# Layer B's shared values: each matmul over 128 contraction rows becomes two over 64, in banks of their own

## The chip, the core and the metric

The kernel runs on one core of one Trainium2 chip. Its engines work side by side and meet at semaphores: PE (TensorE) multiplies, and loads its stationary operand with separate instructions (PEld); ScalarE is ACT in the profile, VectorE DVE, GpSimd POOL, and SP issues the transfers of weights. The metric is the device time of one execution in microseconds; smaller is better.

## The reference, cut to what matters

The model is a two-layer encoder trunk over 256 tokens of width 2048. Layer A is a chunked softmax attention beside an attention into 256 memory tokens, then an MLP with squared ReLU. After it one key and one value projection are made for layer B, whose stick-breaking attention uses them:

```python
kv = rms_norm(h, norm_kv) @ w_kv_shared          # [256, 2048] @ [2048, 3072]
k_sb = split_heads(kv[..., :W_MAIN], N_HEADS_MAIN)   # 12 heads of 128
v_sb = split_heads(kv[..., W_MAIN:], N_HEADS_MAIN)   # 12 heads of 128
```

The change concerns `v_sb` alone: a product of [256, 2048] with [2048, 1536], scaled for each token by the inverse root of its mean square.

## The kernel before, in words

All weights pass once through the chip as a stream of 512 KB pieces, called half-units here. `prepare` (L135) loads one, ACT rounds it to float32r (`hi`, L150) and DVE takes the rest of it (`lo`, L151); four buffers hold each of them. The activations are split in the same way, so a product is the sum of three matmuls: hi by hi, hi by lo, lo by hi. All of these have one line in the profile, L56, since a helper issues PE's instructions in the order in which they are written. The order on ACT, DVE and POOL is set by a scheduler that works with estimated times.

`tokens_major` (L190) makes 512 columns for all 256 tokens. It has a PSUM bank for each of the two tiles of 128 tokens (m = 0, 1) and goes over eight half-units; each holds two tiles of 128 contraction rows. For each of these and each m there are three matmuls with 512 moving columns, so a group has 96. The stationary operand is the activations (`kvx`), the moving one the weights. The banks come from `ps_mm` (L98), which has four, the tiles `acc`; so one group's banks are emptied while the next group fills the other two.

Layer B's shared values (L820 to L825) are three such groups. Ahead of them stands the last down projection of layer A's MLP, behind them the shared keys; both go by `features_major` (L233), one bank for each output tile, emptied by ACT (`low`, L259) and DVE (`dn`, L732, or `sc`, L830). `value_heads` (L380) empties a value group: ACT reads a bank, multiplies by the token's factor `r` and writes the SBUF tile `vb` (L383). Within the first group stand a few small matmuls of two side tasks: `stat` (sums of squares) and `spread` (the factors on all partitions).

Of the kernel before, what the change touches and what calls it, by code (L numbers as in the profile page):

```python
# [16 lines left out]
P = 128  # L17
# [12 lines left out]

# Columns of the small per-partition parameters.
G_ATTN0, G_ATTN1, G_MEM0, G_MEM1, G_MLP0, G_MLP1, G_KV = (16 * i for i in range(7))
G_QK = 7 * 16
N_SMALL = G_QK + 6

# The order of contraction tiles in the output projection: memory heads first.
WO_ORDER = [12, 13, 14, 15] + list(range(12))
AHEAD = 3
# Output tiles of the output projection that begin before the last heads are done.
FIRST = 4  # L40
# Tiles of hidden features that begin before the last residual tile is done.
FIRST_UP = 2
# [3 lines left out]
class InOrder:  # L46
    """An engine whose instructions are issued in the order in which they are written."""

# [20 lines left out]
def trunk(  # L69
# [32 lines left out]

# [1 line left out]
    nc.scalar.preload_act_table_set("natural_log_exp_and_others")  # L104
    # The tensor engine's clock rises while it works: it multiplies zeros until the data arrive.
    zeros = wide.tile([P, 512], F32, name="zeros", tag="wide")
# [11 lines left out]
    neg_tri = const.tile([P, P], F32, name="neg_tri")  # L118
    # neg_tri[k, s] = -1 where k >= s
    nc.gpsimd.affine_select(  # L120
        out=neg_tri[:], in_=neg_ones[:], pattern=[[-1, P]], compare_op=ALU.is_ge,
        fill=0.0, base=0, channel_multiplier=1,
    )
    # Exact in float32r: the sums that they make of a split operand are float32's.
    neg_tri_r = const.tile([P, P], F32R, name="neg_tri_r")
# [3 lines left out]

# [1 line left out]
    stream = []  # L131
# [28 lines left out]

# [1 line left out]
    waiting = deque()  # L162
# [27 lines left out]
    def tokens_major(act, evacuate):  # L190
        """Eight half-units of 512 columns: out[tokens, 512] for both tiles of tokens."""
        banks = [ps_mm.tile([P, 512], F32, name="acc", tag="acc") for _ in range(2)]
        for half in range(8):
            hi, lo = weights()
            for k2 in range(2):
                kt = 2 * half + k2
                h512 = hi[:, k2 * 512 : (k2 + 1) * 512]
                l512 = lo[:, k2 * 512 : (k2 + 1) * 512]
                for m in range(2):
                    a_hi = act[:, kt, m * P : (m + 1) * P]  # L200
                    a_lo = act[:, kt, T + m * P : T + (m + 1) * P]
                    mm(banks[m][:], a_hi, h512, kt == 0, False)
                    mm(banks[m][:], a_hi, l512, False, False)
                    mm(banks[m][:], a_lo, h512, False, kt == KT - 1)
            if half == 7:
                evacuate(banks)
            slot()

    def half_unit(bank, act, order, first, last):
        hi, lo = weights()  # L210
        for k8 in range(8):
            kt = order[k8]
            w = slice(k8 * P, (k8 + 1) * P)
            mm(bank[:], hi[:, w], act[:, kt, :], first and k8 == 0, False)
            mm(bank[:, T:], lo[:, w], act[:, kt, :T], False, last and k8 == 7)

    def one_bank(act, evacuate):
        """As features_major, all parts in the same columns."""
        bank = ps_mm.tile([P, 512], F32, name="acc", tag="acc")
        for half in range(2):  # L220
            hi, lo = weights()
            for k8 in range(8):
                kt = 8 * half + k8
                w = slice(k8 * P, (k8 + 1) * P)
                mm(bank[:, :T], hi[:, w], act[:, kt, :T], kt == 0, False)
                mm(bank[:, :T], hi[:, w], act[:, kt, T:], False, False)
                mm(bank[:, :T], lo[:, w], act[:, kt, :T], False, kt == KT - 1)
            if half == 0:
                slot()
        evacuate(bank)  # L230
        slot()

    def features_major(act, evacuate, order=tuple(range(KT))):  # L233
        """Two half-units of 128 columns: out[features, tokens], and beside it its low part."""
        bank = ps_mm.tile([P, 512], F32, name="acc", tag="acc")
        half_unit(bank, act, order[:8], True, False)
        slot()
        half_unit(bank, act, order[8:], False, True)
        evacuate(bank)
        slot()  # L240

    def halves_first(act, n, evacuate, order=tuple(range(KT)), between=None):
        """n tiles as of features_major, of all of them the first half before the second."""
        banks = []
        for _ in range(n):
            bank = ps_mm.tile([P, 512], F32, name="acc", tag="acc")
            half_unit(bank, act, order[:8], True, False)
            banks.append(bank)
            slot()
        if between is not None:  # L250
            between()
        for i in range(n):
            half_unit(banks[i], act, order[8:], False, True)
            evacuate(i, banks[i])
            slot()
# [5 lines left out]

# [1 line left out]
    def pin(ins, pinned=True):  # L263
        """Work that could be done early, and would then hold up what is more urgent."""
        if pinned:
            tc.keep_in_program_order(ins)

    def split_scaled(dst, kt, src, gain, pinned=False):
        """dst[:, kt] = the high and the low part of src * gain."""
        g = sm[:, gain + kt : gain + kt + 1]  # L270
# [26 lines left out]
    def token_stats(acc, name):  # L297
        """Per token, on partitions: mean square + eps, and its inverse root."""
        ps = ps_y.tile([P, 512], F32, name="stat", tag="y")
# [12 lines left out]
    def spread(r, scale, name):  # L312
        """r of a token, on all partitions along the free dimension."""
        ps = ps_y.tile([P, 512], F32, name="spread", tag="y")
# [10 lines left out]
    def inverse_square(acc, name):  # L325
        """1 / (mean square + eps) of a token, on all partitions."""
        ps = ps_y.tile([P, 512], F32, name="inv", tag="y")
# [6 lines left out]
    def normed_heads(banks, eps_ms, gain, dst):  # L334
        """Four heads of a QK-normed projection: dst[d, head, token]."""

# [54 lines left out]
    def soft_tail(p, spans, rs, vt, j, y, head, ready=None, lag=1):  # L391
        """Normalise p[q, k], transpose it, and weigh the values with it. spans: of each tile of
        queries, its columns in p."""
        for m, (lo, hi) in enumerate(spans):
            nc.vector.tensor_scalar_mul(p[:, lo:hi], p[:, lo:hi], rs[:, m : m + 1])
        n = spans[-1][1]
        tp = None
        blocks = []  # (key tile, query tile, columns in p)
        for m, (lo, hi) in enumerate(spans):
# [80 lines left out]
    def strict(t):  # L480
        """Keep t[s, t] where s < t, in the two diagonal blocks of [0:256 | 128:256]."""
        v = t.rearrange("p (b t) -> p b t", t=P)[:, 0:3:2, :]
# [56 lines left out]

# [1 line left out]
    def wide_group(w):  # L541
# [45 lines left out]

# [1 line left out]
    def spaced(fn, n, per, start=0):  # L589
# [10 lines left out]
    def later(fn, n):  # L600
        """fn, n slots from now."""

# [75 lines left out]

    # q's gains carry the scores' scale
    gq = const.tile([P, 3], F32, name="gq")  # L680
# [5 lines left out]
    def out_proj(l, y, resid, done):  # L686
        """h = resid + y @ w_o, in place in resid; done(o) follows each tile of features."""

# [60 lines left out]

# [1 line left out]
    def x_stat_side():  # L751
# [7 lines left out]
    for j in range(NM):  # L759
        queue_side(mem_head(qm, km[0], vm[0], j, y, 2), 4)  # L760
    # The values come last: only their weighing is left when the last group is done.
    for i in range(3):
# [42 lines left out]

# [1 line left out]
    qx = new_act("qx")  # L807
# [14 lines left out]
    for g in range(3):  # L822
        v_ = heads4(f"vb{g}")
        tokens_major(kvx["xg"], lambda b: value_heads(b, bst["r"], v_))
        vb.append(v_)  # L825
# [15 lines left out]
    for hd in range(NH):  # L841
        q = nar.tile([P, T], F32, name=f"qb{hd}", tag="qb", bufs=3)
        features_major(qx, lambda b: scaled(b, q[:], bst["rbs"]))
        # The last heads are due sooner.
        wait, *lags = (1, 2, 2) if hd < NH - 2 else (0, 2, 2) if hd < NH - 1 else (0, 2, 1)
# [17 lines left out]
def _wide(w):  # L863
    """[2048, n] -> [n / 512, 8, 128, 1024]: of 512 columns, two tiles of rows."""
    k, n = w.shape
# [3 lines left out]
def _narrow(w, order=None):  # L869
    """[k, n] -> [n / 128, k / 1024, 128, 1024]: of 128 columns, eight tiles of rows."""  # L870
    k, n = w.shape
# [6 lines left out]
def _tokens(x):  # L878
    """[256, 2048] -> [4, 128, 1024]: features on partitions, four tiles of them a chunk."""
    return x.T.reshape(4, 4, P, T).transpose(0, 2, 1, 3).reshape(4, P, 1024)  # L880
# [45 lines left out]
```

## Time and profile before

| | |
|---|---|
| time, median of 3 runs | 2241.86 us (2240.25 to 2244.43) |
| the profiled execution: span from first to last instruction | 2249.5 us |
| PE busy | 2233.1 us, 99% |
| DVE, ACT, POOL busy | 58%, 48%, 29% |
| DMA | 184 GB/s mean |
| the three groups of shared values in the span | 1175.09 to 1241.31 us |

The profiled execution has no time beside its span; the span is 7.6 us (0.34%) above the median of the runs, and nothing is known of it outside the span. The span counts from the first to the last instruction. A timeline row gives start, duration, engine, line, operation and how many were merged; in brackets stands the idle time of the engine before it and what ended that. The ends of matmuls are modelled, so the distance between two starts (the pitch) tells what one costs in a stream, and not its duration.

### The profile page before, as it was taken

Reading aid. Unit: us, or ns where it says so; the run is one execution under the profiler, and the core shown is the slowest. Engines: PE = TensorE matmul, PEld = TensorE weight load, DVE = VectorE, ACT = ScalarE, POOL = GpSimd, SP = SyncE. Lnnn points to the kernel's source line nnn. Section 1 sums busy time; section 2 is a strip of 40 time slices with the busy share of each in tenths; the row PEclk is TensorE's granted clock in tenths of the full one; section 3 lists DMA queues with packets and bytes.
Section 4 is the critical chain, followed back from the end, with each engine's and each line's share of the span. In section 5 each row is a group of like instructions: output and inputs, shape, how many; then the busy total and the mean of one; then the engine's idle time right before and its main releaser. Section 6 shows DMA issues by size and latency. Waiting matters only on the chain.

```text
span 2249.5 us, 31961 instructions
## 1 busy us (share of the span) xinstructions
PE 2233.1 (99%) x12208; PEld 1921.3 (85%) x12208; DVE 1304.7 (58%) x1574; ACT 1075.6 (48%) x1572; POOL 652.9 (29%) x662
## 2 busy tenths in 40 slices
PE   8999999999999999999999999999999999999999
PEld 6888888888888888888888888888888888888888
DVE  8755556665555555555665455576555555555554
ACT  6545455544444444444455447554444444444443
POOL 6610112622222222222460112362222222222222
PEclk9999999999999999999999999999999999999999
DMA  7555555555555555555555553455555555555553
GB/s 282 189 176 160 181 177 201 191 187 186 187 187 181 186 187 187 185 185 186 183 188 189 188 185 132 141 196 184 183 186 187 187 182 187 186 185 187 187 194 134
DMA packets 117225, 414.76 MB, mean 184 GB/s; under 512 B 13136, under 2 KB 16720, under 8 KB 117072
## 3 DMA queue, kind: packets, MB, share of 16 engines
q1 hardware_dynamic: 116496, 410.63, 55.0%
q8 instruction: 95, 1.56, 0.3%
q10 hardware_dynamic: 576, 2.10, 0.3%
q14 instruction: 58, 0.48, 0.1%
HBM read 410.58 MB, written 2.10 MB: 183 GB/s over the span
## 4 chain that ended last, share of the span: by engine, by line
PE 97%; issue 1%; DVE 1%; POOL 1%; ACT 0%; DMA 0%; SPq 0%
PE acc L56 94%; PE yp L56 1%; PE tp L56 1%; PE z L56 1%; PE s L56 1%; POOL hid L720 1%; DVE mg L273 0%; DVE lo L151 0%; DMA raw<-in_w_mem 0%; ACT hi L150 0%; ACT hid L719 0%; PE stat L56 0%; PE inv L56 0%; PE spread L56 0%; DVE dn L740 0%
## 5 line engine op out<-in xcount | busy, mean ns | idle before, releaser
L151 DVE TENSOR_TENSOR lo<-raw,hi 128x1024 fp32r<-128x1024 f32 (+1 forms) x771 | 981.3, 1273 | 846.0 <-ACT hi L150 845.4
L150 ACT CAST hi<-raw 128x1024 fp32r<-128x1024 f32 (+1 forms) x771 | 807.2, 1047 | 1117.9 <-PE acc L56 643.3
L56 PE MATMUL acc<-hid,hi 128*128 128x512 f32 (+1 forms) x2064 | 725.3, 397 | 3.5 <-POOL hid L720 3.5
L56 PE MATMUL acc<-mlpx,hi 128*128 128x512 f32 x2048 | 723.9, 399 | 0.0
L56 PE MATMUL acc<-hid,lo 128*128 128x256 f32 x2048 | 575.2, 281 | 0.0
L56 PE MATMUL acc<-mlpx,lo 128*128 128x256 f32 x2048 | 574.9, 281 | 0.0
L56 PEld LDWEIGHTS acc<-hid,hi 128*128 128x128 f32 x2064 | 386.7, 188 | 100.9 <-POOL hid L720 6.1
L56 PEld LDWEIGHTS acc<-mlpx,hi 128*128 128x128 f32 x2048 | 384.8, 188 | 95.7
L56 PEld LDWEIGHTS acc<-hid,lo 128*128 128x128 f32 x2048 | 386.9, 189 | 0.0
L56 PEld LDWEIGHTS acc<-mlpx,lo 128*128 128x128 f32 x2048 | 386.8, 189 | 0.1
L720 POOL TENSOR_TENSOR hid<-upsq,hid 128x256 fp32r<-128x256 f32 x128 | 186.2, 1455 | 546.6 <-ACT hid L719 546.6
L733 POOL TENSOR_TENSOR dn<-dn,r_mlp 128x256 f32<-128x256 f32 x127 | 93.9, 739 | 477.0 <-DVE dn L732 477.0
L56 PE MATMUL acc<-hi,xg 128*128 128x512 f32 x640 | 210.5, 399 | 0.0
L56 PE MATMUL acc<-y,hi 128*128 128x512 f32 x512 | 179.0, 395 | 0.0
L56 PE MATMUL acc<-y,lo 128*128 128x256 f32 x512 | 141.9, 277 | 0.0
L56 PEld LDWEIGHTS acc<-hi,xg 128*128 128x128 f32 x640 | 120.2, 188 | 24.6
L56 PE MATMUL acc<-lo,xg 128*128 128x512 f32 x320 | 124.7, 390 | 0.0
L259 ACT COPY low<-acc 128x256 f32<-128x256 f32 x311 | 113.7, 366 | 4.4 <-PE acc L56 4.4
L56 PEld LDWEIGHTS acc<-y,hi 128*128 128x128 f32 x512 | 96.0, 188 | 21.8
L734 POOL TENSOR_TENSOR h<-h,dn 128x256 f32<-128x256 f32 x127 | 93.7, 738 | 10.0
L56 PEld LDWEIGHTS acc<-y,lo 128*128 128x128 f32 x512 | 96.2, 188 | 0.1
L56 PE MATMUL acc<-hi,mg 128*128 128x512 f32 x256 | 82.1, 398 | 2.1 <-ACT hi L150 1.4
(154 smaller groups left out, 1820.5 us busy)
## 6 DMA issues: line engine op xcount, KB each, us to landing
raw<-in_w_up SPq DMA_DIRECT2D x256, 512.0 KB, 3.4
raw<-in_w_down SPq DMA_DIRECT2D x256, 512.0 KB, 3.3
raw<-in_w_in SPq DMA_DIRECT2D x80, 512.0 KB, 3.4
raw<-in_w_o SPq DMA_DIRECT2D x64, 512.0 KB, 3.4
raw<-in_w_mem SPq DMA_DIRECT2D x29, 512.0 KB, 4.1
raw<-in_w_kv_v SPq DMA_DIRECT2D x24, 512.0 KB, 3.4
raw<-in_w_kv_k SPq DMA_DIRECT2D x24, 512.0 KB, 3.4
raw<-in_w_q SPq DMA_DIRECT2D x24, 512.0 KB, 3.3
```

Of the source, the lines that this page charges most:

```text
L56: return self._tc.keep_in_program_order(fn(*args, **kwargs))
L150: nc.scalar.copy(hi[:, part], raw[:, part])
L151: nc.vector.tensor_tensor(lo[:, part], raw[:, part], hi[:, part].bitcast(F32), op=ALU.subtract)
L259: nc.scalar.copy(low[:], bank[:, T:])
L720: nc.gpsimd.tensor_tensor(hid[:, f, T:], a[:], hid[:, f, :T].bitcast(F32), op=ALU.subtract)
L733: nc.gpsimd.tensor_tensor(t[:], t[:], inv["r2"][:], op=ALU.mult)
L734: nc.gpsimd.tensor_tensor(h(o), h(o), t[:], op=ALU.add)
```

## The change

For the three groups of shared values `tokens_major` is replaced by `tokens_major_rows`, and `value_heads` by `value_heads_rows`. The new loop takes four banks. Each former matmul becomes two: one multiplies the upper 64 contraction rows (partitions 0 to 63) and writes banks 0 or 1 (for m = 0, 1), the other the lower 64 (partitions 64 to 127) and writes banks 2 or 3. Each of them still has 512 moving columns and a stationary operand of 128 columns. To empty them, ACT scales a lower bank into an SBUF tile `vpart`, and DVE scales the upper bank and adds `vpart`. The diff also takes out comments and docstrings, which changes no instruction; line numbers grow by up to 34.

```diff
+    def tokens_major_rows(act, evacuate):
+        banks = [ps_mm.tile([P, 512], F32, name="acc", tag="acc") for _ in range(4)]
+        rows = (slice(0, 64), slice(64, P))
+        for half in range(8):
+            hi, lo = weights()
+            for k2 in range(2):
+                kt = 2 * half + k2
+                cols = slice(k2 * 512, (k2 + 1) * 512)
+                for m in range(2):
+                    a_hi = slice(m * P, (m + 1) * P)
+                    a_lo = slice(T + m * P, T + (m + 1) * P)
+                    for a, w, first, last in (
+                        (a_hi, hi, kt == 0, False),
+                        (a_hi, lo, False, False),
+                        (a_lo, hi, False, kt == KT - 1),
+                    ):
+                        for u, r in enumerate(rows):
+                            mm(banks[2 * u + m][:], act[r, kt, a], w[r, cols], first, last)
+            if half == 7:
+                evacuate(banks)
+            slot()
+
+    def value_heads_rows(banks, r, dst):
+        for m in range(2):
+            s = r[:, 2 * m : 2 * m + 1]
+            part = wide.tile([P, 512], F32, name="vpart", tag="wide")
+            nc.scalar.activation(part[:], banks[2 + m][:], AF.Copy, scale=s)
+            nc.vector.scalar_tensor_tensor(
+                out=dst[:, m * 512 : (m + 1) * 512], in0=banks[m][:], scalar=s, in1=part[:],
+                op0=ALU.mult, op1=ALU.add,
+            )
...
-        tokens_major(kvx["xg"], lambda b: value_heads(b, bst["r"], v_))
+        tokens_major_rows(kvx["xg"], lambda b: value_heads_rows(b, bst["r"], v_))
```

The order of instructions and the semaphores that they wait on show where a bank is waited for. First PE at the start of the first group, behind the last matmuls of the down projection (`hid`), before the change:

```order
L56 MATMUL acc<-hid_3_9059,lo_10695 128x256
L56 MATMUL acc<-hi_10716,kvx 128x512 [waits Activation_49]
L56 MATMUL acc<-lo_10717,kvx 128x512 [waits DVE_49]
L56 MATMUL acc<-hi_10716,kvx 128x512
L56 MATMUL acc<-hi_10716,kvx 128x512 [waits PE_49]
L56 MATMUL acc<-lo_10717,kvx 128x512
```

And with the change:

```order
L56 MATMUL acc<-hid_3_9059,lo_10695 128x256
L56 MATMUL acc<-hi_10716,kvx 128x512 [waits Activation_49]
L56 MATMUL acc<-hi_10716,kvx 128x512 [waits DVE_49,PE_49]
L56 MATMUL acc<-lo_10717,kvx 128x512 [waits DVE_49]
L56 MATMUL acc<-lo_10717,kvx 128x512
L56 MATMUL acc<-hi_10716,kvx 128x512 x2
L56 MATMUL acc<-hi_10716,kvx 128x512 [waits DVE_49] x2
L56 MATMUL acc<-lo_10717,kvx 128x512 x2
```

The seventh and the eighth matmul (m = 1, upper and lower rows) now wait on DVE: their banks are those of the last two tiles of the down projection, which `dn` on DVE empties. Before, the group took the other two banks. (The shape printed is that of the output.)

Second, PE at the start of the second group with the change:

```order
L56 MATMUL acc<-hi_10948,kvx 128x512 x2
L56 MATMUL acc<-hi_10980,kvx 128x512 [waits Activation_49]
L56 MATMUL acc<-hi_10980,kvx 128x512 [waits DVE_49]
L56 MATMUL acc<-lo_10981,kvx 128x512 x2
L56 MATMUL acc<-hi_10980,kvx 128x512 x2
L56 MATMUL acc<-hi_10980,kvx 128x512 [waits Activation_49]
L56 MATMUL acc<-hi_10980,kvx 128x512 [waits DVE_49]
```

For each m the upper rows get a bank that ACT has read in the first group, and the lower rows one that DVE has read. Before, the second group began so:

```order
L56 MATMUL acc<-hi_10898,kvx 128x512
L56 MATMUL acc<-hi_10918,kvx 128x512 [waits Activation_49]
L56 MATMUL acc<-lo_10919,kvx 128x512 [waits DVE_49]
L56 MATMUL acc<-hi_10918,kvx 128x512 x2
L56 MATMUL acc<-lo_10919,kvx 128x512
```

There the waits are those for `hi` and `lo` of the half-unit.

Third, DVE at the end of the first group, before and with the change (`qx` is the split of layer B's queries' input):

```order
L322 TENSOR_SCALAR rbs_b<-rb_b 128x256
L151 TENSOR_TENSOR lo_10950<-raw_10948,hi_10949 128x1024
L273 SCALAR_TENSOR_TENSOR qx<-h_3119,sm,qx 128x256
L151 TENSOR_TENSOR lo_10970<-raw_10968,hi_10969 128x1024
L273 SCALAR_TENSOR_TENSOR qx<-h_3119,sm,qx 128x256
```

```order
L356 TENSOR_SCALAR rbs_b<-rb_b 128x256
L151 TENSOR_TENSOR lo_11024<-raw_11022,hi_11023 128x1024
L307 SCALAR_TENSOR_TENSOR qx<-h_3119,sm,qx 128x256
L151 TENSOR_TENSOR lo_11056<-raw_11054,hi_11055 128x1024
L238 SCALAR_TENSOR_TENSOR vb_10805<-acc,r_b,vpart 128x512 x2
L307 SCALAR_TENSOR_TENSOR qx<-h_3119,sm,qx 128x256
```

The two additions stand right behind the `lo` of a half-unit, where DVE had nothing of the group's end before. On ACT the two reads of the lower banks stand where the two reads of `value_heads` stood.

## The prediction

> **What bounds the kernel now.** First the page: the shares of the engines, and the shares of the chain of work that ended last.
>
> ```profile
> span 2249.5 us, 31961 instructions
> PE 2233.1 (99%) x12208; PEld 1921.3 (85%) x12208; DVE 1304.7 (58%) x1574; ACT 1075.6 (48%) x1572; POOL 652.9 (29%) x662
> PE 97%; issue 1%; DVE 1%; POOL 1%; ACT 0%; DMA 0%; SPq 0%
> ```
>
> PE is the bound, and the chain lies on it. Then whom PE waits for, over the whole span:
>
> ```profile
> PE acc L56 <- DVE lo L151: 5.6, 5, 2.3
> PE acc L56 <- POOL hid L720: 3.5, 8, 0.4
> PE cold L56 <- DVE zeros L107: 1.5, 1, 1.5
> PE acc L56 <- ACT hi L150: 1.4, 1, 1.4
> PE acc L56 <- ACT mg L271: 0.7, 1, 0.7
> ```
>
> That is 12.7 us, and no row is a wait for a PSUM bank. So whatever PE loses in the changed stage is lost at the end, and only what PE does there can win. Then what a matmul of that stage costs, from PE's timeline in the second and third group and at the keys behind them:
>
> ```profile
> 1217.74 0.39 PE L56 MATMUL acc<-lo,kvx 128*128 128x512 f32 x1
> ...
> 1219.33 0.62 PE L56 MATMUL acc<-hi,kvx 128*128 128x512 f32 x2
> 1219.78 0.39 PE L56 MATMUL acc<-lo,kvx 128*128 128x512 f32 x1
> ...
> 1241.31 0.39 PE L56 MATMUL acc<-kvx,hi 128*128 128x512 f32 x1
> ...
> 1241.65 0.40 PE L56 MATMUL acc<-kvx,hi 128*128 128x512 f32 x1
> ```
>
> From 1217.74 to 1219.78 there are nine matmuls: 2.04 / 9 = 226.7 ns each, the pitch, whatever the 0.39 us of a record. In the keys a matmul of 512 columns and one of 256 take 1241.65 - 1241.31 = 0.34 us together here (0.35 us further on), so 256 columns cost some 120 ns: a matmul is about 107 ns for each 256 columns and some 13 ns that do not grow with them.
>
> **The change part by part.** *The rate.* 288 matmuls of 128 rows become 576 of 64 rows with the same 512 columns. If the upper and the lower half of the array run at the same time, a pair costs one pitch; if not, two. No row of the trace has a matmul of 64 rows, so the bounds are these. Below: the fixed 13 ns vanish for each of 288 pairs, -3.7 us. Above: twice the pitch, 288 x 0.2267 = +65.3 us. Between them lies the load of the stationary operand, of which there are now two in a pitch. Its price shows where the moving operand is tiny, with two columns:
>
> ```profile
> 1185.75 0.39 PE L56 MATMUL acc<-hi,kvx 128*128 128x512 f32 x1
> 1185.98 0.50 PE L56 MATMUL stat<-ones,kvsq 128*128 128x2 f32 x4
> 1186.34 0.48 PE L56 MATMUL acc<-hi,kvx 128*128 128x512 f32 x1
> 1186.66 0.39 PE L56 MATMUL acc<-lo,kvx 128*128 128x512 f32 x1
> ```
>
> Four loads with their tiny matmuls take 1186.34 - 1185.98 = 0.36 us, 90 ns each. Two make 180 ns, below the pitch of 227 ns, so they fit if they are loaded beside the streaming, as they are now:
>
> ```profile
> 1198.02 0.39 PE L56 MATMUL acc<-lo,kvx 128*128 128x512 f32 x1
> 1198.02 0.41 PEld L56 LDWEIGHTS acc<-hi,kvx 128*128 128x128 f32 x2
> ```
>
> The load for the next matmul starts with the matmul before it, on the same 128 rows. The Trainium skill, "TensorE: Matmul & The Clock Gate", Part 3 (the mechanism), says that matmuls on different row groups overlap, started some 4 ns apart; no row here can show it. The same place says that a load overlaps a matmul in flight only when the row groups differ; the two rows above disagree, for the undivided array. I take one pitch for a pair, a rate term of 0: the streams lie on separate rows and separate banks, the instructions of a pair are adjacent, and two loads fit. If loads do not quite hide, two of them with the cost of 120 ns that the matmul of 256 columns bounds make 240 ns: 13 x 288 = +3.8 us, the upper end of this case.
>
> *The waits for banks.* A group now takes all four, so nothing covers the emptying. What ACT and DVE do at the three starts and at the start of the keys:
>
> ```profile
> 1175.17 1.06 ACT L150 CAST hi<-raw 128x1024 fp32r<-128x1024 f32 x1 [0.84 <-PE acc L56]
> 1176.12 0.36 ACT L259 COPY low<-acc 128x256 f32<-128x256 f32 x1
> ...
> 1197.37 1.31 ACT L383 ACTIVATE vb<-acc,r_b 128x512 f32<-128x512 f32 x2 [1.05 <-PE acc L56]
> ...
> 1219.07 1.37 ACT L383 ACTIVATE vb<-acc,r_b 128x512 f32<-128x512 f32 x2 [0.99 <-PE acc L56]
> ...
> 1240.83 1.37 ACT L383 ACTIVATE vb<-acc,r_b 128x512 f32<-128x512 f32 x2 [0.99 <-PE acc L56]
> ```
>
> ```profile
> 1176.26 1.23 DVE L151 TENSOR_TENSOR lo<-raw,hi 128x1024 fp32r<-128x1024 f32 x1 [0.64 <-ACT hi L150]
> 1177.40 0.42 DVE L732 TENSOR_TENSOR dn<-acc,low 128x256 f32<-128x256 f32 x1
> ...
> 1196.36 1.22 DVE L151 TENSOR_TENSOR lo<-raw,hi 128x1024 fp32r<-128x1024 f32 x1 [1.55 <-ACT hi L150]
> ```
>
> Start of the first group. Its first matmul starts at 1175.09, and its eighth needs the bank of the last down tile. Three pitches on, at 1175.77, that bank is still full: `low` and `dn` stand behind the rounding of a half-unit on ACT and its rest on DVE, and `dn` ends at 1177.40 + 0.42 = 1177.82. From a release to the next matmul I add 0.2 us, an estimate: a load's 0.09 us and about as much for the semaphore (ACT starts 0.08 us after the first group's 1175.09). Stall: 2.25 us. DVE's and ACT's order there is as before but for one split of `kvx`, which costs nothing: PE needs it seven half-units later.
>
> Start of the second and third group. The row that has its second start at 1219.33 + 0.227 puts the third group's first matmul at 1219.56; a group of 96 pitches (21.76 us) earlier is 1197.80 for the second, and 1241.31 is the keys'. ACT's read of the first bank (690 ns each, below) begins when m = 0 has its last matmul, four before the end, and DVE's addition follows it:
>
> ```profile
> L383 ACT ACTIVATE vb<-acc,r_b 128x512 f32<-128x512 f32 x5 | 3.4, 690 | 3.0 <-PE acc L56 3.0
> ...
> L351 DVE TENSOR_TENSOR qn<-acc,sroot 128x512 f32<-128x512 f32 x20 | 13.7, 686 | 8.0 <-POOL sroot L349 8.0
> L504 DVE SCALAR_TENSOR_TENSOR sp<-z,e 128x384 f32<-128x384 f32 x12 | 6.7, 558 | 7.3 <-ACT e L502 7.3
> ```
>
> The addition (128x512, a bank and an SBUF tile) is not in the trace; the same operation on 384 columns takes 558 ns and another on a full bank 686 ns, so 0.69 us. DVE is free: its `lo` ends at 1197.58. Second group: 1197.37 + 0.69 + 0.04 + 0.69 = 1198.79, with 0.2 us 1198.99, against 1197.80: 1.19 us. Third: 1219.07 + 1.42 + 0.2 = 1220.69 against 1219.56: 1.13 us. The second bank of lower rows comes free 0.69 us after the first and is needed three pitches, 0.68 us, after it: nothing more. Start of the keys: their first bank is one that ACT alone reads, 1240.83 + 0.69 + 0.2 = 1241.72 against 1241.31: 0.41 us. What is late behind these stalls is PE alone: ACT, DVE and the transfers run ahead of it and gain slack. Sum of the stalls: 4.98 us.
>
> *Switching.* The array goes between whole and halved at the first group's start, around `stat` and `spread`, and at the keys, six times, the last under a stall. Each can cost between nothing and what a record outlasts the pitch, 0.39 - 0.23 = 0.16 us; five at the middle make 0.4 us. The Trainium skill, "TensorEngine Tiling (Array Packing)", Key Properties, says that a change of tiling mode drains the engine, which is the upper end.
>
> *ACT and DVE.* ACT's two reads for each group remain; DVE gets six additions, 4.1 us on an engine with 58%, and only those in the stalls count.
>
> Sum: 0 + 4.98 + 0.4 = +5.4 us. On the profiled execution that is 2249.5 + 5.4 = 2254.9 us of span. The span is 7.6 us above the runs' median of 2241.86, and the change adds the same to both: **2247.3 us**.
>
> **The rivals.**
>
> *The halves run one after the other.* For it: the trace has never two matmuls in one pitch; against it, nothing but the rows and banks being separate. The rate adds 65.3 us. A group's m = 0 then ends 0.91 us earlier before its end, and three pairs last 1.36 us: the stalls fall by 0.9 twice, by 0.7 and by 0.4, to 2.1 us. With switching: +67.8, **2309.7 us**.
>
> *The loads are not hidden behind the own half's stream.* A half then alternates between load and stream, 90 + 227 = 317 ns for a pair. For it: nobody knows whether a halved array has room for a second operand; against it, the overlap of the whole array above. It adds 288 x 0.09 = 25.9, with stalls and switching +31.3: **2273.2 us**. The Trainium skill's rule on loads, quoted above, is this rival. Its measured gain of 3.07 for four row tiles, in "Measured speedup vs the span model" on the same page, would mean for a pair 227 x 4 / 3.07 = 295 ns, an estimate near this rival.
>
> *The fixed part of a pitch vanishes, and DVE gives the banks up earlier.* With two streams side by side one half's change of operand lies behind the other's stream: -3.7 us. It decides once a pair costs under 224 ns, since 0.9 us already brings the sum to the edge of what can be told from nothing. For it: the 13 ns; against it: both halves start together, and so change together. Sum 4.98 + 0.4 - 3.7 = +1.7, **2243.5 us**: not slower by what can be measured, and below the median if the switching is free and the hops take less.
>
> **How the numbers follow.** Changes within 0.2%, 4.5 us, cannot be told from none. Chances: pairs at one pitch 0.64, loads not hidden 0.14, one after the other 0.16, fixed part gone 0.06. The first, with rates from -1 to +3.8 us and stalls and switching from 4 to 6.5 us, spans +3 to +10: of its 0.64 some 0.20 lie within 4.5 us. The last gives 0.03 to faster and 0.03 to the same. Together: slower 0.44 + 0.14 + 0.16 = 0.74, the same 0.23, faster 0.03. For the range I keep the first case, the last and the loads, and leave the serial one out: from 2241 to 2276 us. The likeliest case's own range is 2245 to 2252.
>
> **What would show it.** In the changed stage: pairs of 64-row matmuls whose pitch is 0.22 to 0.24 us for a pair (0.45 us: serial; 0.32 us: loads); the stage, from the first matmul on `kvx` to the first of the keys, at 66.2 us before, at 71 to 72 us; four waits of PE, for `dn` (2.2 us), for the additions (1.1 us, twice) and for ACT's `vpart` (0.4 us), and no others beside those of before. The forecast is wrong if the pitch of a pair leaves 0.21 to 0.25 us, or if `dn` moved ahead of the `lo` on DVE.

## The result: 0.22% slower, and where it went

| | before | with the change |
|---|---|---|
| median of 20 runs | 2246.16 us | 2249.84 us |
| ratio, 95% interval | | 1.0022 (1.0012 to 1.0031) |
| span of the profiled execution | 2249.5 us | 2251.1 us |
| the stage: first matmul on `kvx` to the first of the keys | 66.22 us | 71.81 us |

2246.16 x 0.0022 is +4.9 us, between +2.7 and +7.0; the stage alone grew by 5.59 us. The spans differ by only 1.6 us because the rest of the program, which has the same instructions, varies: up to the stage this execution took 1172.40 us where the one before took 1175.09, and behind it 1006.9 where that took 1008.2. So I measure by the stage. Its ends, in PE's timeline with the change:

```profile
1172.40 0.50 PE L56 MATMUL acc<-hi,kvx 64*128 64x512 f32 x2
1172.74 0.40 PE L56 MATMUL acc<-lo,kvx 64*128 64x512 f32 x2
1172.98 0.62 PE L56 MATMUL acc<-hi,kvx 64*128 64x512 f32 x3
1175.10 0.50 PE L56 MATMUL acc<-hi,kvx 64*128 64x512 f32 x1 [1.50 <-DVE dn L766]
1175.10 0.73 PE L56 MATMUL acc<-lo,kvx 64*128 64x512 f32 x2
1175.44 0.85 PE L56 MATMUL acc<-hi,kvx 64*128 64x512 f32 x4
...
1244.21 0.50 PE L56 MATMUL acc<-kvx,hi 128*128 128x512 f32 x1
```

Two matmuls of a pair start together ("x2" with the length of one). Where one half had to wait alone, the other then runs one matmul ahead of it (`hi` and `lo` together at 1175.10). Within a group the pitch of a pair is that of a whole matmul before:

```profile
1197.03 0.62 PE L56 MATMUL acc<-hi,kvx 64*128 64x512 f32 x4
...
1197.71 0.39 PE L56 MATMUL acc<-hi,kvx 64*128 64x512 f32 x2
1198.26 0.50 PE L56 MATMUL acc<-hi,kvx 64*128 64x512 f32 x1 [0.16 <-ACT vpart L237]
1199.05 0.50 PE L56 MATMUL acc<-hi,kvx 64*128 64x512 f32 x1 [0.29 <-DVE vb L238]
1199.05 0.73 PE L56 MATMUL acc<-lo,kvx 64*128 64x512 f32 x2
1199.39 0.85 PE L56 MATMUL acc<-hi,kvx 64*128 64x512 f32 x4
```

From 1197.03 to 1197.71 there are three pairs: 0.68 / 3 = 227 ns. Then the second group starts: its first upper matmul when ACT has read a bank, its first lower one at 1199.05, 1.11 us after it was due (1197.71 + 0.227). The next pair follows 0.34 us later where a pitch is 0.23. Whom PE waited for, over the span:

```profile
PE acc L56 <- DVE lo L151: 6.9, 4, 2.3
...
PE acc L56 <- DVE dn L766: 1.5, 1, 1.5
PE acc L56 <- DVE vb L238: 0.6, 2, 0.3
PE acc L56 <- ACT vpart L237: 0.2, 1, 0.2
```

The last three rows are new. They understate: a wait is counted from the modelled end of the last matmul, and the loss from when the next was due. The `vpart` row is the upper half's wait at 1198.26, which costs nothing of its own, as the lower half comes later. At the keys no wait is listed, but ACT's read of their bank ends 0.05 us ahead of their first matmul (it starts at 1243.47 and takes 0.69 us; the matmul starts at 1244.21). The chain of waits, in order of time, goes through the emptying at both starts (a piece is its start, its length and what it is):

```profile
1197.52 0.70 ACT vpart L237
...
1198.24 0.76 DVE vb L238
...
1199.05 21.41 PE acc L56 x185
...
1220.47 0.70 ACT vpart L237
...
1221.20 0.76 DVE vb L238
...
1222.00 21.44 PE acc L56 x185
```

The stage's growth, term by term, from such rows: 2.1 us at the first start (the eighth matmul came at 1175.10 and was due at 1172.74 + 2 x 0.23 = 1173.20, and 0.11 at each of the two slow first pitches), 1.2 us at the second, 1.2 us at the third, 0.3 us at the keys, and around `stat` and `spread` 0.28 and 0.39 us. For the latter, `stat`:

```profile
1185.20 0.39 PE L56 MATMUL acc<-hi,kvx 64*128 64x512 f32 x1
1185.52 0.61 PE L56 MATMUL stat<-ones,kvsq 128*128 128x2 f32 x4
...
1186.39 0.40 PE L56 MATMUL acc<-lo,kvx 64*128 64x512 f32 x2
```

From the last matmul ahead of it to the second pair behind it are 1.19 us; before the change 1186.66 - 1185.75 = 0.91 us. All six terms make 5.5 us, and the stage grew by 5.59. At the keys the slow first pitch (1244.21 to 1244.55) lies behind the stage as it is counted here.

### The profile page after: what moved, and what is told of

Read it like the earlier page. It is cut to its first block, busy times and chain, and to the rows that moved or that the text cites. A ratio compares the mean times of both kernels' runs of the same rounds, so it can differ in the third digit from the quotient of the medians.

```text
span 2251.1 us, 32544 instructions
## 1 busy us (share of the span) xinstructions
PE 2232.8 (99%) x12496; PEld 1919.3 (85%) x12496; DVE 1309.1 (58%) x1580; ACT 1075.6 (48%) x1572; POOL 652.5 (29%) x662
## 4 chain that ended last, share of the span: by engine, by line
PE 97%; issue 1%; DVE 1%; POOL 1%; ACT 0%; DMA 0%; SPq 0%; DVEq 0%; ACTq 0%
PE acc L56 94%; PE yp L56 1%; PE tp L56 1%; PE z L56 1%; PE s L56 1%; POOL hid L754 1%; DVE lo L151 0%; DVE mg L307 0%; DMA memc<-in_mem_t 0%; DMA raw<-in_w_mem 0%; ACT hi L150 0%; ACT hid L753 0%; ACT vpart L237 0%; DVE vb L238 0%; PE stat L56 0%
```

## The experiments

Stages are from the first matmul on `kvx` to the first of the keys, in one profiled execution each. Timed ratios are to executions of the kernel before that were timed beside them. The first three kernels change the waits for banks, the next three what the array does, the last four the order and size of the halved matmuls.

**Whole matmuls over four banks.**

```diff
-                    for a, w, first, last in (
-                        (a_hi, hi, kt == 0, False),
-                        (a_hi, lo, False, False),
-                        (a_lo, hi, False, kt == KT - 1),
-                    ):
-                        for u, r in enumerate(rows):
-                            mm(banks[2 * u + m][:], act[r, kt, a], w[r, cols], first, last)
+                    for a, w, u, first, last in (
+                        (a_hi, hi, 0, kt == 0, False),
+                        (a_hi, lo, int(kt < KT - 1), kt == 0, kt == KT - 1),
+                        (a_lo, hi, int(kt == KT - 1), False, kt == KT - 1),
+                    ):
+                        mm(banks[2 * u + m][:], act[:, kt, a], w[:, cols], first, last)
```

> Matmuls over all 128 rows again, 96 a group, but spread over the four banks: a bank of each pair takes the first and third matmul of three, the other the second (in the last contraction tile the first two and the third). The emptying is that of the change. The changed stage, from the first matmul on kvx to the first of the keys, took 66.2 us before and 71.8 us with the change. Theory (the loss is in the waits for banks, not in the halving): PE stalls again, 1.7 us at the first group's start, some 0.9 us at each of the next two and 0.3 us at the keys, with 0.1 us for each restart, and nothing for switching: the stage takes 70 to 71 us. Rival (the halving itself, by its rate or its switching, makes the loss, and the waits are hidden): 66.2 to 67 us.

Measured: 1174.97 to 1245.38, 70.4 us; timed 1.0014 (1.0002 to 1.0027). The stall at the first start stands in its PE timeline:

```profile
1175.43 0.61 PE L56 MATMUL acc<-hi,kvx 128*128 128x512 f32 x2
1177.74 0.50 PE L56 MATMUL acc<-lo,kvx 128*128 128x512 f32 x1 [1.70 <-DVE dn L765]
```

So 4.2 of the 5.6 us come with the four banks and their emptying, without a halved matmul. The rival falls.

**The first group whole.**

```diff
-        tokens_major_rows(kvx["xg"], lambda b: value_heads_rows(b, bst["r"], v_))
+        if g == 0:
+            tokens_major(kvx["xg"], lambda b: value_heads(b, bst["r"], v_))
+        else:
+            tokens_major_rows(kvx["xg"], lambda b: value_heads_rows(b, bst["r"], v_))
```

> The first of the three groups goes back to whole matmuls with two banks and to the old emptying; the second and third stay halved. Theory (waits for banks): the 1.9 us wait for the last down tile's bank is gone, and the 0.7 us at stat and spread; the second group's start waits only for ACT's reads, 0.3 to 0.5 us in place of 1.2; the third's 1.1 us and the keys' 0.4 us stay: the stage takes 68 to 68.5 us. Rival (the loss is spread evenly over the halved matmuls): two thirds of 5.6 us stay, 69.9 us.

Measured: 1174.54 to 1242.61, 68.1 us; timed 1.0005 (0.9989 to 1.0022). The loss went from 5.6 to 1.9 us by taking one of three groups back: it belongs to the starts and the side tasks, and is not spread over the matmuls.

**The lower banks complete earlier.** In the last half-unit:

```diff
+                        if half == 7:
+                            mm(banks[m][:], act[:, kt, a], w[:, cols], first, last)
+                            continue
                         for u, r in enumerate(rows):
-                            mm(banks[2 * u + m][:], act[r, kt, a], w[r, cols], first, last)
+                            end = last or (u == 1 and half == 6 and k2 == 1 and a == a_lo)
+                            mm(banks[2 * u + m][:], act[r, kt, a], w[r, cols], first, end)
```

> The last half-unit of each group is multiplied whole, into the upper banks, so the lower banks are complete 2.7 us before the group's end and ACT can read them while PE works. Theory (ACT's read and DVE's addition, one after the other, make the wait at the second and third start): ACT's 0.69 us leaves the wait, which falls from 1.1 us to about 0.4 us at both, and the 0.3 us at the keys goes; three more switches within the groups cost 0.1 to 0.2 us each; the first start keeps its 1.9 us: the stage takes 70 to 70.5 us. Rival (the wait is for something else, such as the end of PE's own work): no change, 71.8 us.

Measured: 1174.18 to 1245.04, 70.9 us, 0.95 us below the change; timed 1.0035 (1.0023 to 1.0047). PE's list of waits has no row of `vpart` or `vb` any more, and the keys start without delay. At the second and third start the first bank is no longer late, but the second still is: the load for the eighth matmul waits for DVE, and the matmul comes at 1201.03, 0.18 us after it was due:

```profile
1201.03 0.18 PEld L56 LDWEIGHTS acc<-hi,kvx 64*128 64x128 f32 x1 [0.23 <-DVE vb L242]
```

ACT had put the rounding of a half-unit between its two reads, which start at 1196.57 and 1198.14. With the slow first pitch behind it, that is 0.3 us at each of the two starts, in place of 1.2. What came in place of the rest is switching, at the end of the first group for instance:

```profile
1196.76 0.81 PE L56 MATMUL acc<-hi,kvx 64*128 64x512 f32 x3
1197.41 0.40 PE L56 MATMUL acc<-lo,kvx 128*128 128x512 f32 x1
```

A pair starts at 1196.76, the first whole matmul, merged with it, comes next, and the second whole one starts at 1197.41. Two pitches, 0.45 us, have become 0.65: 0.2 us, and about as much on the way back, at or above the most that I had put in. The theory of the wait holds; as a repair it returns less than it looks. Its timed ratio is higher than the stage says (4.6 us is 0.21%), just outside the interval; I have no cause for that, the rest of the program being the same.

**The upper rows alone.** `tokens_major` and `value_heads` as before, on `slice(0, 64)` of both operands; the lower rows' part of the values is left out.

> Only the upper 64 contraction rows are multiplied, with two banks a group and the old emptying: 288 matmuls of 64 rows. The lower rows' part of the values is left out. Theory (a matmul of 64 rows costs a full pitch of 227 ns, and its twin on the other rows nothing): 66.2 us and about 1 us for the switching: 67 us. Rival (a lone half is cheaper than a whole, and a pair is bound by something that the two share): clearly below 66 us, down to 33 us if the price goes with the rows.

Measured: 1176.37 to 1290.04, 113.7 us, neither of the two. The windows of its stage (time, PE's busy time and matmuls, granted clock, DMA share, GB/s) show why:

```profile
1180.00:1190.00 10.00, 10.00 (x46) 1.00 0.56 200
1190.00:1200.00 10.00, 10.00 (x27) 0.53 0.33 105
1200.00:1220.00 20.00, 20.00 (x49) 0.50 0.31 106
...
1290.00:1300.00 10.00, 10.00 (x50) 0.85 0.31 107
```

For the first 14 us a lone half matmul has the full pitch, as the theory says:

```profile
1181.08 0.61 PE L56 MATMUL acc<-hi,kvx 64*128 64x512 f32 x2
...
1181.76 0.61 PE L56 MATMUL acc<-hi,kvx 64*128 64x512 f32 x2
```

Three matmuls in 1181.76 - 1181.08 = 0.68 us: 227 ns. At 1190 the granted clock halves and stays at 0.50, though PE never pauses, and comes back some 3 us after whole matmuls have begun. Of four executions three took 2299 to 2302 us and one 2252 us. A whole and a pair kept the full clock; so what the clock goes by is not only whether matmuls follow one another.

**Two thirds.** Of the three products two are made of the upper rows alone and one of both halves; the lower rows' part of two products is left out.

```diff
...
+                    mm(banks[m][:], act[rows[0], kt, a_hi], hi[rows[0], cols], kt == 0, False)
+                    mm(banks[m][:], act[rows[0], kt, a_hi], lo[rows[0], cols], False, False)
+                    for u, r in enumerate(rows):
+                        mm(
+                            banks[2 * u + m][:], act[r, kt, a_lo], hi[r, cols],
+                            u == 1 and kt == 0, kt == KT - 1,
+                        )
```

> Of the three products of a block the first two are made of the upper rows alone, and only the third of both halves; the lower rows' part of two products is left out. The matmuls on upper rows keep one pitch each. With the upper rows alone the clock fell to half 14 us into the stage. Theory A (the clock falls because half of the array's rows stand idle, and two thirds of the work is enough, as in the mix of whole and halved matmuls, which did its last 90 us at full clock with PE streaming for 62% of the time): full clock, 71 to 73 us. Theory B (any stretch of matmuls on 64 rows alone lets it fall): half clock for most of the stage, 110 us or more.

Measured: the profiled execution kept the full clock, 69.8 us from 1175.85. That is below the 71 to 73 us of Theory A: the lower banks are now needed two matmuls later, and the wait for `dn` is 1.0 us in place of 1.5. Of eight timed ones five took 2250 to 2256 us and three 2307 to 2309 us. Both theories are half right: with two thirds of the work the clock falls in some executions and not in others. In 20 executions of the change, where both halves always work, none was above 2257 us.

**Switching.** Two products of each block in halves, the third whole:

```diff
...
+                    mm(banks[m][:], act[:, kt, a_lo], hi[:, cols], False, kt == KT - 1)
```

> Of the three products of a block the third is multiplied whole, into the upper bank, and the other two in halves: the array goes from halves to whole and back 96 times a stage. Theory (each such round trip costs what it costs around stat and spread, 0.28 to 0.39 us by the trace of the change): 71.8 + 96 x 0.28 to 0.39 = 99 to 109 us. Rival (a switch is free, and what is lost there is due to stat and spread themselves): 72 us.

Measured: 1169.26 to 1295.32, 126.1 us, in an execution of 2306 us; the only other one took 2361 us, with a mean granted clock of 0.960 in place of 0.989. In the profiled one the clock fell to 0.50 some 4 us after the start, until 1217, and then was full, for 78 us (not 90, as the expectation for two thirds has it):

```profile
1249.52 0.50 PE L56 MATMUL acc<-hi,kvx 64*128 64x512 f32 x2
1249.86 0.40 PE L56 MATMUL acc<-lo,kvx 64*128 64x512 f32 x2
1250.18 0.94 PE L56 MATMUL acc<-hi,kvx 128*128 128x512 f32 x3
1250.96 0.40 PE L56 MATMUL acc<-lo,kvx 64*128 64x512 f32 x2
```

A block takes 1250.96 - 1249.86 = 1.10 us at full clock, where three pitches are 0.68: 0.42 us for a round trip, a little above what `stat` and `spread` cost (0.28 and 0.39). Of it 0.09 us lie ahead of the whole matmul (1250.18 - 1249.86 = 0.32) and 0.33 us around the first pair behind it (1250.96 - 1250.18 = 0.78, for two pitches). 96 of these make 105.6 us; the 44 us at half clock and the waits make up the rest. The rival, that a switch is free, falls.

**Order.** The same matmuls, by threes, sixes and twelves: in a block of six (twelve, 24) all the upper ones are written ahead of the lower ones. The edit for threes; for the others the loop over `rows` stands one and two levels further out:

```diff
-                    for a, w, first, last in (
...
-                        for u, r in enumerate(rows):
+                    for u, r in enumerate(rows):
+                        for a, w, first, last in (
...
                             mm(banks[2 * u + m][:], act[r, kt, a], w[r, cols], first, last)
```

> The same 576 matmuls on halves, but within a block of six the three upper ones come first and then the three lower ones. Theory (the two halves of the array stream side by side, but matmuls start in the order in which they are written): of six only the third and the fourth overlap, so a block takes four pitches, 0.907 us, in place of three: the stage of 96 blocks grows by 21.8 us to about 92 us. Rival (a lower matmul may start ahead of upper ones written before it): 71.8 us as with the change. Second rival (halves overlap only where adjacent matmuls share a moving tile): no overlap at all, 131 us and the waits.

> The 576 matmuls on halves with six upper ones and then six lower ones (for one contraction tile, both m). With three and three the stage took 71.8 us, as with pairs, so a lower matmul does start ahead of upper ones written before it. Theory A (each half works off its own matmuls, and PE looks ahead far enough): again 71 to 72 us. Theory B (it looks ahead only a few matmuls): of twelve only one pair overlaps in order, eleven pitches for six, so up to 66.2 x 11 / 6 = 121 us, and in between if some of them overlap.

> As before, with twelve upper ones and then twelve lower ones (a half-unit). Theory A (PE looks ahead far enough for 24 matmuls and their 24 loads): 71 to 72 us. Theory B (the window ends between three and twelve): up to 66.2 x 23 / 12 = 127 us.

Measured: 1168.36 to 1240.19, 71.8 us; 1176.08 to 1249.95, 73.9 us; 1174.49 to 1275.16, 100.7 us; timed 1.0023 (1.0000 to 1.0047), 1.0027 (1.0009 to 1.0045) and 1.0132 (1.0080 to 1.0184). With threes my theory of starts in written order falls, as does the second rival of no overlap (131 us), and the first rival holds: the stage is that of the pairs, and in its first row two matmuls on `hi` start together, which are the first and the fourth written:

```profile
1168.36 0.51 PE L56 MATMUL acc<-hi,kvx 64*128 64x512 f32 x2
1168.70 0.41 PE L56 MATMUL acc<-lo,kvx 64*128 64x512 f32 x2
```

With twelves it is in between. From the start of that kernel's stage:

```profile
1174.49 0.49 PE L56 MATMUL acc<-hi,kvx 64*128 64x512 f32 x1
1174.83 0.39 PE L56 MATMUL acc<-lo,kvx 64*128 64x512 f32 x1
1175.06 0.63 PE L56 MATMUL acc<-hi,kvx 64*128 64x512 f32 x2
1175.53 0.38 PE L56 MATMUL acc<-lo,kvx 64*128 64x512 f32 x1
1175.75 0.62 PE L56 MATMUL acc<-hi,kvx 64*128 64x512 f32 x2
1176.22 0.39 PE L56 MATMUL acc<-lo,kvx 64*128 64x512 f32 x1
1176.45 0.62 PE L56 MATMUL acc<-hi,kvx 64*128 64x512 f32 x3
1176.79 0.51 PE L56 MATMUL acc<-lo,kvx 64*128 64x512 f32 x2
```

Eight upper matmuls start one after the other, and then, within the "x3" of 1176.45, the first lower one, the thirteenth written, beside the ninth and tenth. So PE starts a matmul on the other half about three places ahead of its turn. With sixes it is the same: the seventh written starts beside the third, at 1176.64. Later the pattern repeats every 1.96 us (rows at 1180.74, 1182.70 and 1184.65), 8.6 pitches for a run of twelve, so that some 3.4 overlap at each change of half. To cost nothing, a run of six needs an overlap of three and a run of three 1.5. The threes lose nothing against the pairs; the 2.1 us that the sixes lose are not explained by this.

**Half the columns.** Each matmul on a half has 256 columns, twice as many of them:

```diff
-                        for u, r in enumerate(rows):
-                            mm(banks[2 * u + m][:], act[r, kt, a], w[r, cols], first, last)
+                        for c in (0, T):
+                            part = slice(cols.start + c, cols.start + c + T)
+                            for u, r in enumerate(rows):
+                                mm(
+                                    banks[2 * u + m][:, c : c + T], act[r, kt, a], w[r, part],
+                                    first and c == 0, last and c == T,
+                                )
```

> Each matmul on a half has 256 moving columns in place of 512, so there are twice as many, and a pair's two loads of the stationary operand stand against a stream of about 107 ns in place of 213. Theory (the two halves load side by side as they stream): a pair takes what a whole matmul of 256 columns takes, 120 to 127 ns: 576 pairs take 69 to 73 us in place of 65.3, and the stage 76 to 80 us. Rival (loads go one after the other, 90 ns each, and were hidden only behind 512 columns): 180 ns a pair, the stage about 110 us.

Measured: 1171.08 to 1246.26, 75.2 us; timed 1.0041 (1.0016 to 1.0067). In its steady part twelve matmuls, six pairs, take 0.72 us:

```profile
1177.10 0.76 PE L56 MATMUL acc<-hi,kvx 64*128 64x256 f32 x8
...
1177.82 0.76 PE L56 MATMUL acc<-hi,kvx 64*128 64x256 f32 x8
```

That is 120 ns a pair, as for a whole matmul of 256 columns, and below two loads in a row at 90 ns. The two halves do load side by side; the rival of serial loads falls with room to spare. The stage is a little under the expected 76 to 80 us; it is 3.4 us above that of the pairs, near the 288 x 13 ns = 3.7 us that twice as many pitches cost.

Two matmuls of a pair into one and the same bank weren't tried, so whether the halves need banks of their own stays open.

## Why the prediction was right, step by step

*The rate, put at 0.* Right: 227 ns for a pair, against 226.7 for a whole one. The two upper ends fall with it: serial halves (0.45 us a pair) and loads that do not hide (0.32 us). In the changed kernel a load still starts with the matmul ahead of it on the same half:

```profile
1197.03 0.19 PEld L56 LDWEIGHTS acc<-hi,kvx 64*128 64x128 f32 x2
```

It starts with the first pair of the row at 1197.03 above. The rule of the Trainium skill, "TensorE: Matmul & The Clock Gate", Part 3, that a load overlaps only a matmul on other row groups, thus does not hold here for a halved array either. The rival that the fixed 13 ns vanish falls too: three pairs take 0.68 us, as three whole matmuls did.

One premise of this term was misread. The 90 ns for a load are a mean over four, the first of which had been loaded ahead. Behind them the loads of the kernel before start 0.11 us apart:

```profile
1186.31 0.19 PEld L56 LDWEIGHTS acc<-hi,kvx 128*128 128x128 f32 x1
...
1186.42 0.19 PEld L56 LDWEIGHTS acc<-lo,kvx 128*128 128x128 f32 x1
```

At that rate two loads in a row would take 0.22 us, not 0.18, and would only just fit into a pitch. That the term is 0 does not rest on this room: the halves load side by side, as the run with half the columns shows.

*The stalls, put at 2.25, 1.19, 1.13 and 0.41 us.* Measured 2.1, 1.2, 1.2 and 0.3, sum 4.8 for 4.98. The waits are those that were forecast, but that the sum comes out so close is in part luck: it was made of errors that nearly cancel. I put 0.2 us between a release and the next matmul, and it is 0.05 us (`dn` ends at 1175.05, the matmul starts at 1175.10):

```profile
1174.63 0.42 DVE L766 TENSOR_TENSOR dn<-acc,low 128x256 f32<-128x256 f32 x1
...
1175.10 0.18 PEld L56 LDWEIGHTS acc<-hi,kvx 64*128 64x128 f32 x1 [1.94 <-DVE dn L766]
...
1175.21 0.65 PEld L56 LDWEIGHTS acc<-hi,kvx 64*128 64x128 f32 x4
```

But the first pitch behind a wait is 0.34 us and not 0.23, which I had not seen, although the trace before has it too (behind its wait for `hid` at 545.02 the next matmul starts at 545.36). The rows fit that: the load of a waiting matmul waits with it, so the next loads start 0.11 us behind it, and not with it as in the stream. And DVE's addition takes longer than its 0.69:

```profile
L238 DVE SCALAR_TENSOR_TENSOR vb<-acc,r_b,vpart 128x512 f32<-128x512 f32 x6 | 4.3, 749 | 1.4 <-ACT vpart L237 1.4
```

*Switching, put at 0.4 us.* Measured 0.7 us around `stat` and `spread`; the 0.1 us at the stage's first pitch are in the 2.1 us above. It was undersized, since I took the middle between nothing and 0.16 us for each change. A round trip is 0.28 to 0.42 us, so a single change costs 0.14 to 0.21 us, around that upper end.

*The sum:* +5.4 us of forecast against 5.59 us in the stage and +4.9 us (2.7 to 7.0) in the timed runs. That it is a loss was a near thing to measure: 0.22% against the 0.2% that can be told from nothing. The forecast time of 2247.3 us stood on a median of three runs, 2241.86 us; over 20 runs the kernel before has 2246.16, so the time came out 2.5 us above the forecast while the growth was right.

## What to carry to other kernels

A stage that gives every PSUM bank to one group pays the whole emptying at each start: what is to be added up is each bank's last write, its reads in turn, and the queue that they stand in, and not the busy share of the engines that read. Splitting the contraction into two halves, with the two of a pair written side by side, costs no rate and wins none; alone, it only uses up banks and adds switching. And a matmul that leaves half of the array's rows idle is not cheaper, and a run of them can halve the clock until whole matmuls follow.

## What was not expected of the hardware

- The granted clock fell from 1.00 to 0.50 while PE streamed without a pause, 14 us after matmuls on 64 rows alone had begun, in three of four executions; with both halves at work in a third of the products, in three of eight; with pairs throughout, in none of 20. It came back some 3 us after whole matmuls had begun. Idle rows alone do not decide: the kernel of the switching experiment has no lone half, but streams for only 0.68 of each 1.10 us, and its clock fell in both executions. By the share of the array's time in use, the cases are a half (three of four fell), 0.62 (two of two), two thirds (three of eight) and, with twelves, 6 pitches of work in 8.6, 0.70 (none of two). That this share decides is argued from these few cases, which ran on two chips, and where the edge lies was not measured.
- Matmuls on different halves do not start in the order in which they are written: the thirteenth started beside the ninth and tenth. The Trainium skill, "TensorE: Matmul & The Clock Gate", Part 3, has matmuls start and end strictly in order; the measurement decides against it for the starts on two row groups.
- Behind a wait the first pitch is 0.34 us, 0.11 us above the others.
- A change between whole and halved matmuls and back costs 0.28 to 0.42 us.
